# A hybrid decoder step: the delta rule's 32x32 blocks substituted on 128 partitions, from the right

## The chip, the cores and the metric

The kernel runs on one core of one Trainium2 chip. The metric is device time in microseconds of one execution; lower is better. Of the core's engines, PE (TensorE) multiplies matrices, DVE (VectorE) and ACT (ScalarE) work on elements, POOL (GpSimd) does small side work, and SP (SyncE) issues most of the DMA transfers. Each engine runs its own queue in order; semaphores tie the queues together.

## The reference

One layer of a decoder with two branches that read one input projection: a gated short convolution (A), and a gated DeltaNet (B) with 8 heads of 128 x 128. They are merged by sigmoid gates and projected out. There are 1024 prompt tokens and 8 samples of one token. The part that the change touches is the delta rule, which needs the inverse of a unit lower triangular matrix in every chunk of every head:

```
a_mat = jnp.where(strict, jnp.einsum('bhncd,bhnsd->bhncs', kb, k) * decay, 0.0)
a_mat = a_mat + jnp.eye(C, dtype=jnp.float32)
rhs = jnp.concatenate([v * beta[..., None], kb * jnp.exp(gc)[..., None]], axis=-1)
sol = lax.linalg.triangular_solve(a_mat, rhs, left_side=True, lower=True, unit_diagonal=True)
...
def step(S, xs):
    v_new = u_c - jnp.einsum('bhcd,bhde->bhce', w_c, S)
    o = jnp.einsum('bhcd,bhde->bhce', qd_c, S) + jnp.einsum('bhcs,bhse->bhce', aqk_c, v_new)
    S = S * gl_c[..., None, None] + jnp.einsum('bhcd,bhce->bhde', kd_c, v_new)
```

## The kernel before, in words

The input projection is a list of jobs of 128 columns each (`run`, line 692). A job has three groups of 344 tokens, each with 8 x 3 matmuls (`pm_t<-xh,whi`, `xl,whi`, `xh,wlo`: both sides are split in a high and a low part), which fill one of four PSUM tiles `pm`. ScalarE or VectorE then evacuates the tile. Weights come in as `wraw` two jobs ahead, and are split by ScalarE (`whi`) and VectorE (`wlo`).

Beside the projection, and between its matmuls, runs the work of the heads as strands (Python generators). `slot` (line 598) is called after every three matmuls and lets each strand whose due time is past issue its next piece. The due times come from a planner (`Sched`, line 60, and `Paced`, line 112): every instruction that is written advances a planned clock of its engine by a cost, a DMA by a latency and its size, and a strand is due when its last result is planned to be there. `sched.loose()` leaves an instruction out of the strand's own chain of due times. So a change of costs, of the number of instructions or of DMAs moves the order of all engines from that point on.

One strand per head is `delta_gen` (line 864). In its order:

- keys and queries (`kq`) are transposed and squared, and the products k·k and k·q of the 8 chunks of 128 tokens come in PSUM tiles `pa`; VectorE multiplies them by the decays into `DB` and `DA`. `DB` holds minus the strict lower triangle A.
- The four 32x32 diagonal blocks of each chunk, 32 blocks a head, go to DRAM (`sA<-DB`, line 935), and come back with one block per partition (`Tt<-sA`, line 942): 32 partitions of 1024 elements. The products `vp` and `qd` are made meanwhile.
- Lines 963 to 973 substitute: for j from 1 to 30, all rows below j add their element of column j times row j, in two VectorE instructions (`Ttmp<-Tt`, `Tt<-Tt,Ttmp`) of (31 - j) x j elements. The result is each block's inverse, whose diagonal is set to one in the middle.
- The inverse goes to DRAM (`sT<-Tt`, line 974) and comes back with rows on partitions (`Tn<-sT`, line 978). VectorE transposes it (`Un<-Tn`), ScalarE copies it into `U` and `T11`, and small matmuls (`Un,DB`, `Tn,Qs`, ...) build the 128x128 inverse.
- The chain over the 8 chunks follows: `X` (VectorE) from the product with the state, `U` x `X` (TensorE), `vn` (ScalarE), then the new state `S` (VectorE). At its end VectorE normalises the output `on`, and TensorE transposes it.

The chain of one head runs while the next head prepares its blocks. Two tiles `raw` hold projected queries, keys and values until VectorE has convolved them (`kq<-raw`, `vT<-raw`); until then the next columns wait in their PSUM tiles.

Of the kernel before, what the change touches and what calls it, by code (L numbers as in the profile page):

```python
# [8 lines left out]
F32 = mybir.dt.float32  # L9
# [3 lines left out]
ALU = mybir.AluOpType  # L13
# [3 lines left out]
P = 128  # L17
D = 1024
NK = 8
S = 1024  # L20
# [133 lines left out]
def hybrid_step(  # L154
# [8 lines left out]
    sched = Sched()  # L163
    V, A, PE, GP, SY = (Paced(e, n, sched) for e, n in (
        (nc.vector, "V"), (nc.scalar, "A"), (nc.tensor, "PE"), (nc.gpsimd, "GP"), (nc.sync, "SY")))
# [12 lines left out]
    def tt(out, a, b, op):  # L178
        V.tensor_tensor(out=out, in0=a, in1=b, op=op)
# [32 lines left out]
    def rsqrt1(x, n):  # L212

        col = lambda t: tp.tile([P, 1], F32, tag=f"rs_{t}", name=f"rs_{t}")[:n]
        y, a, x4, x16 = (col(t) for t in ("y1", "a1", "x4", "x16"))
        ts(y.bitcast(I32), x.bitcast(I32), -0.5, 1597463007.0, ALU.mult, ALU.add)
        ts(x4, x, 0.25)
        ts(x16, x, 0.0625)
        for xs_ in (x, x4, x16):
            ts(a, y, y, xs_, ALU.mult, ALU.mult)  # L220
            stt(y, a, 3.0, y, ALU.subtract, ALU.mult)
        return y
# [45 lines left out]
    sA = dram.tile([NH, NC, 4, 32, 32], F32, name="sA")  # L268
    sT = dram.tile([NH, NC, 4, 32, 32], F32, name="sT")
# [594 lines left out]
    def delta_gen(h, st):  # L864
# [13 lines left out]
        for src, sq in ((0, ssk), (1, ssq)):  # L878
            for half in range(2):
                pt = ps_aux()  # L880
                for i in range(4):
                    c = half * 4 + i
                    transpose(pt[:, i * C:(i + 1) * C], kq[:, src, c * C:(c + 1) * C])
                sched.loose()
                for i in range(4):
                    c = half * 4 + i
# [19 lines left out]
        for half in range(2):  # L906
# [7 lines left out]
            for c2 in (2 * half, 2 * half + 1):  # L914
# [6 lines left out]
                for i in range(2):  # L921
                    c = 2 * c2 + i
# [8 lines left out]
        t_kk = sched.cur.t  # L931
# [3 lines left out]
            SY.dma_start(out=sA[h, :, b].rearrange("c r j -> r c j"), in_=DB[bs, :, bs])  # L935
        while not T4.ready():
            yield
        Tt_ = T4.get("Tt", S)
        Tf = Tt_[:32]
        Tt = Tf.rearrange("p (r j) -> p r j", j=32)  # L940
        tmp = bp.tile([32, 256], F32, tag="Ttmp", name="Ttmp")
        SY.dma_start(out=Tt, in_=sA[h].rearrange("c b r j -> (c b) r j"))
        t_at, sched.cur.t = sched.cur.t, t_kk
        vp = bp.tile([P, NC, C], F32, tag="vp", name="vp", bufs=2)
        for half in range(2):
            pt = ps_aux()
            for i in range(4):
                c = half * 4 + i
# [11 lines left out]
        yield  # L960
        sched.cur.t = max(sched.cur.t, t_at)
        yield 0.0
        for j in range(1, 31):
            n = 31 - j
            tv = tmp[:, 0:n * j].rearrange("p (n w) -> p n w", w=j)
            tt(tv, Tt[:, j + 1:32, j:j + 1].to_broadcast([32, n, j]),
               Tt[:, j:j + 1, 0:j].to_broadcast([32, n, j]), ALU.mult)
            tt(Tt[:, j + 1:32, 0:j], Tt[:, j + 1:32, 0:j], tv, ALU.add)
            if j == 15:
                sched.loose()  # L970
                V.memset(Tf[:, 0:1024:33], 1.0)
                sched.loose(False)
            yield 0.0
        SY.dma_start(out=sT[h].rearrange("c b r j -> (c b) r j"), in_=Tt)
        T4.give(Tt_)
        Tn = bp.tile([P, NC, 32], F32, tag="Tn", name="Tn")
        Un = bp.tile([P, NC, 32], F32, tag="Un", name="Un")
        SY.dma_start(out=Tn, in_=sT[h].rearrange("c b r j -> (b r) c j"))
# [9 lines left out]
        for b in range(2):  # L988
            bs = slice(32 * b, 32 * b + 32)
            A.copy(out=T11[bs, :, bs], in_=Tn[bs])  # L990
        yield
# [8 lines left out]
        for p in (0, 1):  # L1000
# [13 lines left out]
            A.copy(out=U[b1, :, b2], in_=pt[b1, :, 0:32])  # L1014
            A.copy(out=T11[b2, :, 0:32], in_=pt2[b2, :, 0:32])
            yield 0.0
# [7 lines left out]
        for c in range(NC):  # L1024
            PE.matmul(pt[0:64, c, :], lhsT=T11[:, c, :], rhs=Qs[0:64, c, :], start=True, stop=True)
        A.copy(out=U[0:64, :, 64:128], in_=pt[0:64])
# [69 lines left out]
    def head_jobs(h):  # L1096
        st = {}

        def kdst():
            st["kq"] = bp.tile([P, 2, CY], F32, tag="kq", name="kq", bufs=2)  # L1100
            return st["kq"][:, 0, :]

        qkv_job(COL_K + h * P, 8 + h, lambda: h < 2 or flags.get(("done", h - 2)), kdst,
                lambda d: start(decay_gen(h, st)))
        qkv_job(COL_Q + h * P, h, lambda: "kq" in st, lambda: st["kq"][:, 1, :], lambda d: st.update(q=True))

        def vpost(d):
            st["v"] = d
            start(delta_gen(h, st))

        qkv_job(COL_V + h * P, 16 + h, lambda: "q" in st and T4.ready(), lambda: T4.get("vT", CY), vpost)

        return st
# [266 lines left out]
    def alloc(key, side):  # L1380
        pools[key] = tc.alloc_tile_pool(name=key, bufs=1, side=side)
        return pools[key]
# [369 lines left out]
    T4 = Slots(alloc("t4", "left"), "t4", NT4, CY)  # L1752
    bp = tc.alloc_tile_pool(name="bpool", bufs=1, side="left")
# [2 lines left out]
        GP.memset(r_[:, 0:3], 0.0)  # L1756
    U = bp.tile([P, NC, C], F32, name="U")
    T11 = bp.tile([64, NC, 64], F32, name="T11")
    GP.memset(U, 0.0)
    GP.memset(T11, 0.0)  # L1760
    for gi, (g0, gn) in enumerate(GROUPS):
# [55 lines left out]
    for j in range(9):  # L1817
        i, n, xr, mh, ml, held = pre.pop(j)
# [32 lines left out]
        r = rsqrt1(ms_[:n], n)  # L1851
        for half in range(2):
            hs = slice(half * 512, (half + 1) * 512)
            stt(yt[:n, hs], yt[:n, hs], r, xr[:n, hs], ALU.mult, ALU.add)
            out = y_prompt[0, i * P:(i + 1) * P, hs] if i < 8 else y_sample[:, 0, hs]
# [38 lines left out]
```

## Time and profile before

| | before |
|---|---|
| median of 3 runs | 1435.64 us (1431.11 to 1438.38) |
| span of the profiled execution | 1432.3 us |
| substitutions, VectorE busy, 8 heads | 76.1 + 76.2 us |
| granted TensorE clock, mean | 0.998 |

The profiled execution is known by its span, from its first to its last instruction; its own time is not listed apart from the runs. In the profile nearly every instruction has one line, that of the helper at line 121 that records it, so I go by the names of tiles: `out<-in`. A busy PE counts matmuls that overlap each other. "Idle ... <- X" is the time in which an engine had nothing running ahead of an instruction, and what ended it.

### The profile page before, as it was taken

The numbers are of one execution on the slowest core, as the hardware profiler recorded it, in microseconds if no ns is written. First come the engines' busy times: TensorE is split into PE (matmuls) and PEld (weight loads), VectorE is DVE, ScalarE is ACT, GpSimd is POOL, SyncE is SP. The second block draws the span as 40 slices with busy tenths as digits, with TensorE's granted clock in tenths as the row PEclk, the third lists the DMA queues.
The fourth block names the chain that finished last, engine by engine and source line by source line (L and its number), as shares of the span: only waits on it lengthen the run. The fifth ranks groups of instructions, "written<-read, shape, count | busy, mean of one in ns | idle before, by whom it ended". The sixth has DMA issues, their size and how long they took to land.

```text
span 1432.3 us, 25802 instructions
## 1 busy us (share of the span) xinstructions
PE 1401.0 (98%) x10130; PEld 1340.5 (94%) x10130; DVE 984.4 (69%) x2436; ACT 656.4 (46%) x1521; POOL 35.6 (2%) x59
## 2 busy tenths in 40 slices
PE   6999999899999999999999999999999999999997
PEld 4899999899999999999999999999999999999786
DVE  6754867759569585496864924988877867854553
ACT  6766453855528554466383332253323344532211
POOL 0000000100001000000000000000000110000000
PEclk9999999999999999999999999999999999999999
DMA  9523143132422324224132221344711885743221
GB/s 320 144 48 102 54 127 81 54 80 78 119 60 69 94 62 117 50 66 121 54 97 68 79 68 32 118 170 164 243 53 42 236 265 172 244 150 91 92 87 59
DMA packets 181922, 158.59 MB, mean 111 GB/s; under 512 B 25351, under 2 KB 157856, under 8 KB 181794
## 3 DMA queue, kind: packets, MB, share of 16 engines
q1 hardware_dynamic: 177248, 148.43, 35.2%
q0 software_dynamic: 4352, 8.46, 2.0%
q8 instruction: 79, 1.29, 0.4%
q14 instruction: 41, 0.34, 0.1%
q10 hardware_dynamic: 202, 0.08, 0.0%
HBM read 120.25 MB, written 36.91 MB: 110 GB/s over the span
## 4 chain that ended last, share of the span: by engine, by line
PE 84%; DVE 8%; DMA 5%; ACT 1%; issue 1%; SPq 1%; DVEq 0%; ACTq 0%
PE pm_t L121 63%; PE pa_t L121 19%; PE pb L121 2%; DVE acc L121 2%; DVE wlo L121 1%; DMA xs<-in_x_prompt_dram 1%; SPq L121 1%; DMA yraw<-yAsc 1%; DVE Tt L121 1%; DVE kq L121 1%; DMA wor<-in_w_o_dram 1%; DVE Ttmp L121 1%; DVE wr L121 0%; DMA yraw<-yBsc 0%; DMA pa__11678<-yBsc 0%
## 5 line engine op out<-in xcount | busy, mean ns | idle before, releaser
L121 PE MATMUL pm_t<-xh,whi 128*128 128x344 f32 (+1 forms) x1576 | 517.9, 329 | 2.2 <-ACT gate L121 2.2
L121 PE MATMUL pm_t<-xh,wlo 128*128 128x344 f32 (+1 forms) x1576 | 500.4, 318 | 0.0
L121 PE MATMUL pm_t<-xl,whi 128*128 128x344 f32 (+1 forms) x1576 | 500.1, 317 | 0.0
L121 PEld LDWEIGHTS pm_t<-xh,whi 128*128 128x128 f32 x1576 | 297.4, 189 | 4.7 <-ACT gate L121 2.5
L121 PEld LDWEIGHTS pm_t<-xl,whi 128*128 128x128 f32 x1576 | 297.3, 189 | 0.2
L121 PEld LDWEIGHTS pm_t<-xh,wlo 128*128 128x128 f32 x1576 | 296.9, 188 | 0.4
L121 DVE TENSOR_TENSOR wlo<-wraw,whi 128x512 fp32r<-128x512 f32 x136 | 91.8, 684 | 65.2 <-ACT whi L121 63.1
L121 ACT CAST whi<-wraw 128x512 fp32r<-128x512 f32 x136 | 82.7, 623 | 85.6 <-PE pm_t L121 83.6
L121 DVE TENSOR_TENSOR Ttmp<-Tt 32x30 f32<-32x30 f32 (+14 forms) x240 | 76.1, 317 | 14.7 <-DMA Tt<-sA 10.3
L121 DVE TENSOR_TENSOR Tt<-Tt,Ttmp 32x30 f32<-32x30 f32 (+14 forms) x240 | 76.2, 317 | 4.4
L121 ACT CAST whi<-wr 128x1024 fp32r<-128x1024 f32 x42 | 44.0, 1047 | 73.5 <-PE pa_t L121 34.9
L121 DVE SCALAR_TENSOR_TENSOR kq<-raw,vecs,kq 128x528 f32<-128x528 f32 x96 | 69.9, 758 | 1.5 <-ACT kq L121 1.3
L121 PE MATMUL pm_t<-thi,wlo 128*128 128x258 f32 x240 | 67.6, 283 | 1.6 <-DVE wlo L121 1.6
L121 PE MATMUL pm_t<-tlo,whi 128*128 128x258 f32 x240 | 67.6, 282 | 0.0
L121 PE MATMUL pm_t<-thi,whi 128*128 128x258 f32 x240 | 67.6, 282 | 0.0
L121 PE MATMUL pa_t<-thi,whi 128*128 128x258 f32 x224 | 63.3, 282 | 1.1 <-ACT whi L121 1.1
L121 PE MATMUL pa_t<-thi,wlo 128*128 128x258 f32 x224 | 63.4, 283 | 0.8 <-DVE wlo L121 0.8
L121 PE MATMUL pa_t<-tlo,whi 128*128 128x258 f32 x224 | 63.2, 282 | 0.0
L121 PE MATMUL pm_t<-yhi,whi 128*128 128x344 f32 x192 | 61.5, 321 | 0.0
L121 PE MATMUL pm_t<-ylo,whi 128*128 128x344 f32 x192 | 61.4, 321 | 0.0
L121 PE MATMUL pm_t<-yhi,wlo 128*128 128x344 f32 x192 | 61.4, 320 | 0.0
L121 DVE TENSOR_TENSOR wlo<-wr,whi 128x1024 fp32r<-128x1024 f32 x42 | 51.3, 1221 | 8.9 <-ACT whi L121 8.7
(406 smaller groups left out, 2834.0 us busy)
## 6 DMA issues: line engine op xcount, KB each, us to landing
wraw<-in_w_in_dram SPq DMA_DIRECT2D x60, 512.0 KB
wr<-in_w_in_dram SPq DMA_DIRECT2D x40, 256.0 KB
aw<-in_ada_w_dram SPq DMA_DIRECT2D x16, 512.0 KB
gBsc<-gate SPq DMA_DIRECT2D x8, 516.0 KB
gAsc<-gate SPq DMA_DIRECT2D x8, 516.0 KB
txs<-phi SPq DMA_DIRECT2D x8, 516.0 KB
txs<-plo SPq DMA_DIRECT2D x8, 516.0 KB
tlo<-txs POOLq DMA_DIRECT2D x8, 516.0 KB, 7.3
```

The lines of the kernel that those rows point to most:

```text
L121: r = f(*args, **kw)
```

## The change

The rows of the 32x32 blocks are dealt over four groups of 32 partitions: group g holds rows g, g + 4, g + 8, ... of all 32 blocks in a tile `Tw` (128 partitions, 8 rows of 32). `Tw` starts as the identity, copied by GpSimd from a constant `Ti`, and the blocks themselves are loaded four times, once for each group, into `At`. The substitution runs from the right: for j from 31 down to 1, each row adds its element of column j times row j of A to its columns below j. Only rows from 4 * (j // 4) on take part, so an instruction has (8 - j // 4) x j elements per partition, on 128 partitions. There are 31 steps of two instructions in place of 30. Four stores put the rows back in their places in `sT`. `Ttmp` has 80 elements in place of 256. The planned time of the loads now counts from the products (`t_kk`), not from the landing of the sA stores.

```
-        Tt_ = T4.get("Tt", S)
-        Tf = Tt_[:32]
-        Tt = Tf.rearrange("p (r j) -> p r j", j=32)
-        tmp = bp.tile([32, 256], F32, tag="Ttmp", name="Ttmp")
-        SY.dma_start(out=Tt, in_=sA[h].rearrange("c b r j -> (c b) r j"))
+        At_ = T4.get("At", S)
+        At = At_.rearrange("p (r j) -> p r j", j=32)
+        Tw = bp.tile([P, 8, 32], F32, tag="Tw", name="Tw")
+        tmp = bp.tile([P, 80], F32, tag="Ttmp", name="Ttmp")
+        GP.tensor_copy(out=Tw, in_=Ti)
+        sched.cur.t = t_kk
+        for g in range(4):
+            sched.loose(g < 3)
+            SY.dma_start(out=At[32 * g:32 * g + 32], in_=sA[h].rearrange("c b r j -> (c b) r j"))
...
-        for j in range(1, 31):
-            n = 31 - j
+        for j in range(31, 0, -1):
+            r0 = j // 4
+            n = 8 - r0
             tv = tmp[:, 0:n * j].rearrange("p (n w) -> p n w", w=j)
-            tt(tv, Tt[:, j + 1:32, j:j + 1].to_broadcast([32, n, j]),
-               Tt[:, j:j + 1, 0:j].to_broadcast([32, n, j]), ALU.mult)
-            tt(Tt[:, j + 1:32, 0:j], Tt[:, j + 1:32, 0:j], tv, ALU.add)
-            if j == 15:
-                sched.loose()
-                V.memset(Tf[:, 0:1024:33], 1.0)
-                sched.loose(False)
+            tt(tv, Tw[:, r0:8, j:j + 1].to_broadcast([P, n, j]),
+               At[:, j:j + 1, 0:j].to_broadcast([P, n, j]), ALU.mult)
+            tt(Tw[:, r0:8, 0:j], Tw[:, r0:8, 0:j], tv, ALU.add)
             yield 0.0
-        SY.dma_start(out=sT[h].rearrange("c b r j -> (c b) r j"), in_=Tt)
-        T4.give(Tt_)
+        T4.give(At_)
+        for g in range(4):
+            sched.loose(g < 3)
+            SY.dma_start(out=sT[h, :, :, g::4, :].rearrange("c b r j -> (c b) r j"), in_=Tw[32 * g:32 * g + 32])
...
+    Ti = bp.tile([P, 8, 32], F32, name="Ti")
+    GP.memset(Ti, 0.0)
+    for g in range(4):
+        GP.memset(Ti.rearrange("p r j -> p (r j)")[32 * g:32 * g + 32, g:g + 253:36], 1.0)
```

The order moves on every engine from head 0's substitution on. Three places follow.

VectorE, where head 4's first step stands among the chain of head 3 (`X` and `S`), before:

```order
L121 SCALAR_TENSOR_TENSOR S_5804<-S_5747,egl_96,pa_t_5801 128x128
L121 SCALAR_TENSOR_TENSOR X_5823<-pa_t_5819,nx_4427,vp_4741 128x128
L121 SCALAR_TENSOR_TENSOR S_5852<-S_5804,egl_96,pa_t_5849 128x128
L121 TENSOR_TENSOR Ttmp_5760<-Tt_5759 32x30
L121 MEMSET Tt_5759 32x32
L121 TENSOR_TENSOR Tt_5759<-Tt_5759,Ttmp_5760 32x30
L121 TENSOR_TENSOR Ttmp_5760<-Tt_5759 32x58
L121 SCALAR_TENSOR_TENSOR X_5870<-pa_t_5866,nx_4427,vp_4741 128x128
```

and now:

```order
L121 SCALAR_TENSOR_TENSOR S_5899<-S_5851,egl_96,pa_t_5896 128x128
L121 SCALAR_TENSOR_TENSOR X_5917<-pa_t_5913,nx_4457,vp_4709 128x128
L121 SCALAR_TENSOR_TENSOR S_5944<-S_5899,egl_96,pa_t_5941 128x128
L121 SCALAR_TENSOR_TENSOR X_5963<-pa_t_5959,nx_4457,vp_4709 128x128
L121 TENSOR_TENSOR Ttmp_5803<-Tw_5802,At_5801 128x31
L121 TENSOR_TENSOR wlo_6069<-wraw_5738,whi_6023 128x512
L121 TENSOR_TENSOR Tw_5802<-Tw_5802,Ttmp_5803 128x31
```

Counted from head 4's last `DA<-pa_t`, two `X` stood ahead of the first step and the third four rows behind it; now four stand ahead of it, and none follows within the next ten rows.

VectorE again, at the end of head 0's chain, where head 2's convolutions (`kq<-raw`) stand among the steps of the normalisation (`ro`) of head 0's output `on`; `Un` is head 1's, `DB` and `DA` are head 2's decays. Before:

```order
L121 SCALAR_TENSOR_TENSOR ro_y_2930<-ro_a_2931,ro_y_2930 128x8
L121 SCALAR_TENSOR_TENSOR kq_2924<-raw0_719,vecs_82,kq_2924 128x528
L121 TENSOR_TENSOR ro_a_2931<-ro_y_2930 128x8
L121 SCALAR_TENSOR_TENSOR kq_2924<-raw0_719,vecs_82,kq_2924 128x528
L121 SCALAR_TENSOR_TENSOR ro_a_2931<-ro_a_2931,so_2706 128x8
L121 SCALAR_TENSOR_TENSOR kq_2924<-raw1_720,vecs_82,kq_2924 128x528
L121 SCALAR_TENSOR_TENSOR ro_y_2930<-ro_a_2931,ro_y_2930 128x8
L121 SCALAR_TENSOR_TENSOR kq_2924<-raw1_720,vecs_82,kq_2924 128x528
L121 TENSOR_TENSOR on_2705<-on_2705,ro_y_2930 128x1024
L121 TENSOR_TENSOR DB_3091<-DA_3092,m_strict_72 128x1024
```

and now:

```order
L121 SCALAR_TENSOR_TENSOR kq_2933<-raw1_720,vecs_82,kq_2933 128x528
L121 TENSOR_TENSOR ro_a_2940<-ro_y_2939 128x8
L121 STREAM_TRANSPOSE Un_3024<-Tn_3023 128x256
L121 SCALAR_TENSOR_TENSOR ro_a_2940<-ro_a_2940,so_2515 128x8
L121 TENSOR_TENSOR DB_3043<-DA_3044,m_strict_72 128x1024
L121 SCALAR_TENSOR_TENSOR ro_y_2939<-ro_a_2940,ro_y_2939 128x8
L121 COPY qs_s_99<-kq_2933 128x8
L121 TENSOR_TENSOR DA_3044<-DA_3044,m_causal_77 128x1024
L121 TENSOR_TENSOR on_2514<-on_2514,ro_y_2939 128x1024
```

From the last `S` of the chain to `on` there were eleven `kq`; now there are nine, and `Un`, `DB` and `DA` stand ahead of `on`. On TensorE 37 projection matmuls stood between the chain's last product and the transposes of `on`; now 73 do.

SP's queue at head 1, from the stores of its blocks, before:

```order
L121 DMA sA_106<-DB_1754 32x8x32 x4
L121 DMA wraw_3149<-in_w_in_dram 128x8x128
L121 DMA Tt_2489<-sA_106 32x1024
L121 DMA rsc_113<-sm_rT_2595 8x128
L121 DMA rB_2297<-rsc_113 128x1024
```

and now:

```order
L121 DMA sA_106<-DB_1771 32x8x32 x4
L121 DMA At_2496<-sA_106 32x1024 x4
L121 DMA rsc_113<-sm_rT_2681 8x128
L121 DMA wraw_3074<-in_w_in_dram 128x8x128
L121 DMA rB_2392<-rsc_113 128x1024
```

Four loads stand where one stood, and the weight load that stood ahead of it stands behind them.

## The prediction

> **What bounds the kernel now.** I read the page first, then busy time by stage, then who waits on TensorE, then those places row by row.
>
> ```profile
> span 1432.3 us, 25802 instructions
> PE 1401.0 (98%) x10130; PEld 1340.5 (94%) x10130; DVE 984.4 (69%) x2436; ACT 656.4 (46%) x1521; POOL 35.6 (2%) x59
> PE 84%; DVE 8%; DMA 5%; ACT 1%; issue 1%; SPq 1%; DVEq 0%; ACTq 0%
> ```
>
> TensorE is busy 98% of the span and carries 84% of the chain; VectorE, the engine that the change relieves, is busy 69%. A faster VectorE is worth only what TensorE waits for it. The change touches the heads, so I cut the span where the heads begin and end and where TensorE idles. Columns: window, its length, busy time and count of PE, PEld, DVE, ACT, POOL, granted clock, DMA share, GB/s.
>
> ```profile
> 0.00:62.00 62.00, 48.87 (x308) 38.77 (x309) 42.86 (x109) 44.13 (x71) 5.12 (x21) 1.00 0.84 257
> 62.00:264.00 202.00, 202.00 (x1409) 195.63 (x1408) 132.41 (x388) 105.13 (x269) 1.63 (x6) 1.00 0.31 79
> 264.00:276.00 12.00, 8.06 (x77) 7.08 (x76) 12.00 (x28) 11.86 (x24) 2.89 (x2) 1.00 0.12 34
> 276.00:498.00 222.00, 221.95 (x1707) 214.36 (x1707) 155.75 (x457) 124.71 (x365) 7.61 (x7) 1.00 0.30 82
> 498.00:509.00 11.00, 9.00 (x53) 8.72 (x52) 5.24 (x22) 3.08 (x12) 0.00 (x0) 0.84 0.29 74
> 509.00:930.00 421.00, 421.00 (x3136) 411.92 (x3135) 286.50 (x831) 194.68 (x536) 6.74 (x7) 1.00 0.28 79
> 930.00:1433.00 503.00, 490.07 (x3452) 463.98 (x3450) 349.60 (x607) 172.83 (x249) 11.58 (x16) 1.00 0.46 147
> ```
>
> From 62 to 930 us, where all eight heads lie, TensorE idles 3.94 us in one place (264 to 276), 2.00 in another (498 to 509) and 0.05 elsewhere. In the second the granted clock is 0.84, which costs 0.16 x 11 = 1.8 us more. So **the room in the stage of the change is about 7.8 us**, 0.54% of the span. The 13.1 us idle before 62 and 12.9 after 930 lie outside the heads. TensorE's waits of the stage:
>
> ```profile
> PE pm_t L121 <- ACT gate L121: 2.2, 1, 2.2
> PE pa_t L121 <- DVE X L121: 2.0, 1, 2.0
> PE pa_t L121 <- DVE on L121: 1.7, 1, 1.7
> ```
>
> The place at 501 us (a timeline of VectorE, and the window behind it):
>
> ```profile
> 499.28 0.35 DVE L121 SCALAR_TENSOR_TENSOR S<-S,egl,pa_t 128x128 f32<-128x128 f32 x1 [2.20 <-PE pa_t L121]
> 502.81 0.19 DVE L121 TENSOR_TENSOR Ttmp<-Tt 32x30 f32<-32x30 f32 x1 [3.18 <-DMA Tt<-sA]
> 503.40 0.33 DVE L121 SCALAR_TENSOR_TENSOR X<-pa_t,nx,vp 128x128 f32<-128x128 f32 x1
> 503.80:508.40 4.60, 4.60 (x23) 4.60 (x23) 3.37 (x13) 1.24 (x5) 0.00 (x0) 0.63 0.00 0
> ```
>
> The first substitution step of head 4 stands at the front of VectorE's queue and waits 3.18 us for its DMA; X of head 3's chain is queued behind it, and TensorE waits for X. Afterwards the clock is 0.63 for 4.6 us: 0.37 x 4.6 = 1.7 us. **Price of this place: 2.0 + 1.7 = 3.7 us.**
>
> The place at 264 to 276 us (VectorE and TensorE):
>
> ```profile
> 263.04 0.35 DVE L121 SCALAR_TENSOR_TENSOR S<-S,egl,pa_t 128x128 f32<-128x128 f32 x1
> 271.97 1.21 DVE L121 TENSOR_TENSOR on<-on,ro_y 128x1024 f32<-128x1024 f32 x1
> 267.49 0.42 PE L121 MATMUL pm_t<-xh,whi 128*128 128x344 f32 x1 [2.22 <-ACT gate L121]
> 273.23 1.09 PE L121 MATMUL pa_t<-ident,on 128*128 128x128 f32 x8 [1.72 <-DVE on L121]
> 159.58 34.42 PE pm_t L121 x219
> L121 DVE SCALAR_TENSOR_TENSOR kq<-raw,vecs,kq 128x528 f32<-128x528 f32 x96 | 69.9, 758 | 1.5 <-ACT kq L121 1.3
> ```
>
> The last row but one is from the chain of waits: 34.42 / 219 = 0.157 us for each projection matmul. In the order of before, 37 of them stand between head 0's last chain product and the transposes of `on`: 5.8 us of work. VectorE needs 10.1 us from that S to the end of `on` (263.04 to 273.1), most of it eleven convolution instructions `kq` of 0.76 us. The difference, 4.3, is the 3.9 us that TensorE idles: once for a PSUM bank behind a full ScalarE, once for `on`. **Price: 3.9 us**, and the substitution is not in it (it ended at 258); only the order can change it.
>
> **The change, part by part.** *The substitution's instructions.*
>
> ```profile
> L121 DVE TENSOR_TENSOR Ttmp<-Tt 32x30 f32<-32x30 f32 (+14 forms) x240 | 76.1, 317 | 14.7 <-DMA Tt<-sA 10.3
> L121 DVE TENSOR_TENSOR Tt<-Tt,Ttmp 32x30 f32<-32x30 f32 (+14 forms) x240 | 76.2, 317 | 4.4
> L121 DVE TENSOR_TENSOR nx<-cB,egc 128x8 f32<-128x8 f32 x8 | 1.4, 173 | 0.2
> L121 DVE TENSOR_TENSOR Ttmp<-Tt 32x58 f32<-32x58 f32 x16 | 3.3, 207 | 0.5
> L121 DVE TENSOR_TENSOR Ttmp<-Tt 32x84 f32<-32x84 f32 x16 | 3.7, 231 | 0.4
> ```
>
> Before, 60 instructions a head, 152.3 / 8 = 19.0 us. Now 31 steps of two, each of (8 - j//4) x j elements per partition: 8 to 76, mean 1560 / 31 = 50. Eight elements on 128 partitions take 173 ns, 58 on 32 take 207, 84 take 231: the length counts, the partitions do not show. At 50 elements I take 200 ns, bounded by the 173 and 231: 62 x 0.200 = 12.4 us a head (10.7 to 14.3). VectorE loses 6.6 us a head, 53 us in all. On the path this is worth nothing by itself, since the three windows that hold all of the substitutions but the start of head 4's (62 to 264, 276 to 498, 509 to 930) have at most 0.05 us of idle TensorE; it counts through the two places.
>
> *The transfers.*
>
> ```profile
> 405.39 1.82 SPq L121 DMA_DIRECT2D sA<-DB  x4
> 408.45 0.31 SPq L121 DMA_DIRECT2D Tt<-sA  x1
> 185.60 0.32 SPq L121 DMA_DIRECT2D sT<-Tt  x1
> 187.64 0.41 SPq L121 DMA_DIRECT2D Tn<-sT  x1
> 192.73 0.45 DVE L121 STREAM_TRANSPOSE Un<-Tn 128x256 f32<-128x256 f32 x1 [0.88 <-DMA Tn<-sT]
> ```
>
> Four loads for one: 3 x 0.31 = 0.9 us more on SP, so `At` is complete 0.9 to 1.2 us later than `Tt` was. Four stores of 128-byte rows for one of 4 KB rows: the four sA stores, also of 128-byte rows, keep the next load waiting 3.06 us (405.39 to 408.45), the one sT store 2.04 (185.60 to 187.64); so `Tn` comes 1.0 us later, at most 7.1 + 1.0 = 8.1 us behind the last step. Behind SP's extra 1.9 us a head stand weight loads, issued two jobs (2 x 72 x 0.157 = 22.6 us) ahead: hidden; without that cover 1.9 us a head. For `Un` and the ScalarE copies of `Tn` the cover is the distance in the new order: at least 94 projection matmuls (14.8 us) between the last PSUM tile read ahead of the last step and the first product with `Un`. More than 8.1, so nothing.
>
> *The copy of the identity on GpSimd* is not shown before. Its nearest row is a copy of 24 elements:
>
> ```profile
> L121 POOL COPY raw<-hist_q x24: 197/262/3512, 59.5 to 715.7; 128x24 f32<-128x24 f32 x24
> ```
>
> From 0.2 to 3.5 us (least, median, most) for 24 elements; for 256 I bound it by 0.2 and 4 us and take 1. It is issued with the sA stores, some 5 us before `At` lands, and costs nothing; if that cover went, the first step and what VectorE has queued behind it would wait up to 4 us at a head. The setup memsets on GpSimd lie beside the first projection.
>
> *The order.* In the new order the first step of head 4 stands behind two more rounds of X and S of head 3's chain than before. Rounds there are about 4 us apart, so it comes some 8 us later, against 3.18 us of waiting plus 1.2 us of later landing: the wait goes. At the other heads X follows five rows behind the first step at the earliest, and the product that it reads is made later than `At` lands. Term: **-3.7 us** (at worst 0: the wait stays). At head 0's end 73 projection matmuls (11.5 us) now stand where 37 did; VectorE's queue there holds nine `kq` (6.9), `Un` (0.45), two wide decay instructions and `on` (1.2 each, as `on` above), 11.0 us, and half a microsecond of small ones. So the 3.9 us go if the queue keeps time: **-3.9 us**, bounds 0 and -3.9. This end is narrow, and counted the same way those of heads 2, 4 and 6 have 0.4 to 0.5 us to spare (before, heads 2 and 4 had 0.3 and 0.7, and no wait). I charge 0.5 us for each of the four: **+2.0 us**, bounds 0 and 4 x 2.
>
> **Sum:** -3.7 - 3.9 + 2.0 = -5.6 us, so the profiled span would go from 1432.3 to 1426.7. The span is 3.3 us under the median of the runs (1435.64) and inside them (1431.11 to 1438.38); I put the difference on the median: **1430.0 us**.
>
> **The rivals.**
> 1. *All room goes*: both waits vanish, no new one comes, and the shifted transfers after 930 us save a microsecond or two of 12.9. 1435.6 - 7.8 - 1.3 = 1426.5. For it: the counts above; against: four narrow ends.
> 2. *Nothing on balance*: one wait moves to another head, or the short instructions do not get shorter (the change then does not do what it says), and VectorE's load is as before: 1435.6. For it: the narrow ends. Against: the wait at 501 us is gone by a wide margin.
> 3. *Slower: the longer way through sT.* Should the last step run late against TensorE, so that less than 8.1 us lie between it and the first `Un` product, every head pays the 1.0 us of late `Tn` and, as at 503 us, part of a 1.7 us slow clock: 8 x (1.0 + 0.3) = 10.4, so 1446. Against: 14.8 us at the narrowest. The Trainium skill, "DMA: Bandwidth & Descriptors", Specifications, says that transfers under 512 B fall below line rate, with a read-modify-write, which speaks against the four stores. The sA row agrees only so far as 1.0 us.
> 4. *More room than idle time shows.* If TensorE's weight loads, not its matmuls, measure its room, the stage has 868.0 - 837.7 = 30.3 us (PEld of the five windows from 62 to 930), and a freed VectorE could give all of it: 1405. Against: 202.00 of 202 us are busy in a window whose PEld is 195.63, with nothing that waits. The Trainium skill, "Perfetto Trace Analysis", Identifying the Most-Contended Engine, has this rule: matmul busy time is a poor measure of the distance from the limit, weight-load busy share a better one.
>
> **How the numbers follow.** Forecast 0.44, rival 1 0.22, rival 2 0.25, rival 3 0.07, rival 4 0.02. 0.5%, about what a measurement of this kernel can tell from no change, is 7.2 us: below 1428.5 or above 1442.8. A quarter of the forecast's cases lie below 1428.5 (it is 1.5 us above), and nearly all of rival 1's: 0.11 + 0.20 + 0.02 = 0.33 faster; slower 0.08 (rival 3 and a little of rival 2); same 0.59. The range leaves out rivals 3 and 4 and the fringes of 1 and 2: 1422 to 1440.
>
> **What would show it.** Right: DVE busy falls by about 53 us to some 930, steps of 0.17 to 0.23 us; no PE wait for X near head 4's first step, clock 1.00 there; PE idle from 62 to 930 us about 2 us. Wrong: PE waits for `on` of 2 us at several heads, or for `Un`, U or X behind `At` or `Tn`; steps over 0.25 us; a low clock in a new place.

## The result, and the profile after

| | before | after |
|---|---|---|
| median of the runs | 1436.06 us (1431.11 to 1438.38) | 1422.88 us (1422.29 to 1424.44) |
| span of the profiled execution | 1432.3 us | 1420.6 us |
| substitutions, VectorE busy, 8 heads | 76.1 + 76.2 us | 51.9 + 51.9 us |

The ratio is 0.9909, 95% interval 0.9891 to 0.9926: 13.2 us faster, more than twice the 5.6 forecast. Three lines of the page of after (span, busy time, and the chain that ended last by engine):

```profile
span 1420.6 us, 25886 instructions
...
PE 1396.6 (98%) x10130; PEld 1341.2 (94%) x10130; DVE 937.7 (66%) x2444; ACT 658.0 (46%) x1521; POOL 36.5 (3%) x72
...
PE 91%; DVE 5%; DMA 3%; ACT 1%; SPq 0%; issue 0%; DVEq 0%; ACTq 0%
```

VectorE lost 46.7 us (984.4 to 937.7), but TensorE's sum of weight loads is the same (1340.5 and 1341.2) and its busy time fell by only 4.4 of the 11.7 us of the span. The windows of after, in the prediction's columns:

```profile
62.00:264.00 202.00, 201.97 (x1417) 197.12 (x1416) 128.47 (x412) 113.56 (x284) 3.31 (x10) 1.00 0.33 82
264.00:276.00 12.00, 11.95 (x149) 10.92 (x148) 8.67 (x16) 11.76 (x22) 0.20 (x1) 1.00 0.22 71
276.00:498.00 222.00, 221.93 (x1683) 217.27 (x1681) 140.99 (x454) 120.92 (x365) 5.68 (x8) 1.00 0.33 90
498.00:509.00 11.00, 11.00 (x76) 11.00 (x74) 10.83 (x59) 8.40 (x18) 0.00 (x0) 1.00 0.21 54
509.00:930.00 421.00, 420.51 (x3123) 411.29 (x3124) 269.42 (x809) 193.09 (x528) 9.60 (x10) 1.00 0.31 85
930.00:1433.00 503.00, 480.61 (x3387) 454.94 (x3385) 336.50 (x590) 166.11 (x237) 11.58 (x16) 0.99 0.45 143
```

From 62 to 930 us, TensorE idles 0.64 us (6.0 before). The two places are empty, and the clock at 498 to 509 us is 1.00. TensorE's waits that the profile shows between 62 and 930 us (total, times, longest) are these two, the first at the window's edge, and neither for `X`, `Un` or a gate:

```profile
PE pm_t L121 <- ACT last_q L121: 1.1, 1, 1.1
PE pa_t L121 <- DVE on L121: 0.5, 1, 0.5
```

At head 4 (a timeline of VectorE), `X` now runs first, and the first step behind it waits for nothing:

```profile
496.82 0.35 DVE L121 SCALAR_TENSOR_TENSOR X<-pa_t,nx,vp 128x128 f32<-128x128 f32 x1 [1.04 <-PE pa_t L121]
497.19 0.19 DVE L121 TENSOR_TENSOR Ttmp<-Tw,At 128x31 f32<-128x31 f32 x1
```

**Waits inside "busy".** Idle time went down by 7.3 us in the whole span, yet the span by 11.7. So I took the start of every matmul to the start of the next, less the 20th percentile of that interval for the same three neighbours (the matmul ahead, the matmul itself and the next, by PSUM tile and shape) over 15 traces: what is over is lost time, idle or not. Here is that sum by stage, in us:

| | before | after |
|---|---|---|
| ahead of 62 us | 10.8 | 11.0 |
| 62 to 930 us | 21.4 | 11.0 |
| of it waits over 1 us | 6.4 (3) | 0 |
| of it slow clock at 504 to 508 us | 1.7 | 0 |
| of it waits of 0.04 to 0.2 us ahead of products of the heads | 6.1 (70) | 2.8 (33) |
| of it waits of 0.2 to 1 us | 0.2 (1) | 1.1 (3) |
| after 930 us | 13.8 | 12.3 |

The four rows from 62 to 930 us name 14.4 of the 21.4 us before and 3.9 of the 11.0 after. The other 7 us in each are nearly all differences under 0.04 us, which a 20th percentile leaves in any order. The weight loads tell the same: from 62 to 930 us they are busy 837.7 us before and 847.6 after, so the time without one fell from 30.3 to 20.4 us, by 9.9, where idle time fell by 5.35.

The short waits look like this: a timeline of TensorE before, in head 0's chain, with two to four projection matmuls between the links, and VectorE's two rows of `S`.

```profile
252.15 0.32 PE L121 MATMUL pm_t<-xl,whi 128*128 128x344 f32 x1
252.30 0.61 PE L121 MATMUL pa_t<-S,kq 128*128 128x128 f32 x4
252.66 0.40 PE L121 MATMUL pm_t<-xh,wlo 128*128 128x344 f32 x1
...
253.97 0.49 PE L121 MATMUL pa_t<-vn,kd 128*128 128x128 f32 x2
254.30 0.39 PE L121 MATMUL pa_t<-vn,DA 128*128 128x128 f32 x2
254.44 0.40 PE L121 MATMUL pm_t<-xh,wlo 128*128 128x344 f32 x1
254.68 0.32 PE L121 MATMUL pm_t<-xh,whi 128*128 128x344 f32 x1
254.90 0.71 PE L121 MATMUL pa_t<-S,kq 128*128 128x128 f32 x4
255.37 0.40 PE L121 MATMUL pm_t<-xl,whi 128*128 128x344 f32 x1
...
251.63 0.35 DVE L121 SCALAR_TENSOR_TENSOR S<-S,egl,pa_t 128x128 f32<-128x128 f32 x1
254.50 0.35 DVE L121 SCALAR_TENSOR_TENSOR S<-S,egl,pa_t 128x128 f32<-128x128 f32 x1 [0.17 <-PE pa_t L121]
```

The same group takes 0.36 us to the next start at 252.30 and 0.47 at 254.90, where it stands only two projection matmuls behind the product that `S` is made from. The row is 0.1 longer, and the matmul ahead starts 0.22 before it, against 0.15. The `S` that it reads ends at 254.85, 0.05 us ahead of it; that of the group at 252.30 ended 0.32 ahead. Neither wait shows as idle, since the rows overlap.

### The profile page after: what moved, and what is told of

It is laid out like the page before. It is cut to its first block, busy times and chain, and to the rows that moved or that the text cites. A ratio compares the mean times of both kernels' runs of the same rounds, so it can differ in the third digit from the quotient of the medians.

```text
span 1420.6 us, 25886 instructions
## 1 busy us (share of the span) xinstructions
PE 1396.6 (98%) x10130; PEld 1341.2 (94%) x10130; DVE 937.7 (66%) x2444; ACT 658.0 (46%) x1521; POOL 36.5 (3%) x72
## 4 chain that ended last, share of the span: by engine, by line
PE 91%; DVE 5%; DMA 3%; ACT 1%; SPq 0%; issue 0%; DVEq 0%; ACTq 0%
PE pm_t L121 66%; PE pa_t L121 22%; PE pb L121 2%; DVE kq L121 1%; DMA xs<-in_x_prompt_dram 1%; DMA yraw<-yAsc 1%; DMA wor<-in_w_o_dram 0%; DVE S L121 0%; SPq L121 0%; DMA sg<-gAsc 0%; DVE wlo L121 0%; DVE Tw L121 0%; DVE Ttmp L121 0%; DMA sg<-gBsc 0%; DVE ml L121 0%
## 5 line engine op out<-in xcount | busy, mean ns | idle before, releaser
L121 DVE TENSOR_TENSOR Ttmp<-Tw,At 128x60 f32<-128x60 f32 (+24 forms) x248 | 51.9, 209 | 8.8 <-DMA At<-sA 3.7
L121 ACT ACTIVATE junk<-pa_t 128x128 f32<-128x128 f32 x192 | 53.8, 280 | 5.6 <-PE pa_t L121 2.7
```

Source lines behind the costliest of these rows:

```text
L121: r = f(*args, **kw)
```

## The experiments

Fifteen kernels ran. The kernel before, run beside them, gave 1436.4 to 1436.9 us in the medians of four batches.

**The old steps in the new order, and the new steps in the old.** The planner's figures are kept apart from the work: here it counts one substitution while the other is issued.

```
         for j in range(31, 0, -1):
+            for _ in range(2):
+                sched.note("V", 66.0 + (8 - j // 4) * j / 0.96)
+            sched.mute = True
+            i = 31 - j
+            n = 31 - i
...
+                tt(tv, Tt[:, i + 1:32, i:i + 1].to_broadcast([32, n, i]),
+                   Tt[:, i:i + 1, 0:i].to_broadcast([32, n, i]), ALU.mult)
+                tt(Tt[:, i + 1:32, 0:i], Tt[:, i + 1:32, 0:i], tv, ALU.add)
...
+            sched.mute = False
```

> The changed kernel with the 60 substitution instructions of before put back (on partitions 0 to 31), while the planner goes on counting the 62 short ones, and the four loads and four stores stay: new order, old VectorE time (about 19.0 us a head in place of 13.0). Theory O (the order is what brings the gain: the two places and the short waits go because instructions stand elsewhere): as the changed kernel, 1422 to 1426 us, TensorE idle 62 to 930 us under 1.5 us. Theory W (VectorE's shorter queue brings it: X, S and vn come sooner because each step ahead of them is shorter): back to 1433 to 1437 us. A half each: about 1429.

Measured: 1433.24 us (1428.09 to 1442.54), ratio 0.9982 (0.9962 to 1.0002). The two places are gone (11.65 busy of 12 us, 11.00 of 11), but TensorE's waits from 62 to 930 us are new ones:

```profile
PE pm_t L121 <- DVE wlo L121: 2.6, 4, 1.8
PE pa_t L121 <- DVE Un L121: 1.8, 2, 1.4
PE pa_t L121 <- DVE DA L121: 0.9, 1, 0.9
```

So neither theory: the new order alone keeps some 3 of 13 us, and the interval takes in none. The clock has a part in that: the eight runs with a mean clock of 0.996 to 0.998 have the median 1430.9, the four of 0.990 to 0.992 lie at 1437.9 to 1442.5. A second edit was in this kernel: `At` is here what is stored to `sT`, so the pool slot's next user waits for that store, which VectorE does for 3.6 us ahead of `kql`. The double products below are without it. The next kernel turns the exchange round:

```
+        for i in range(1, 31):
+            for _ in range(2):
+                sched.note("V", 66.0 + (31 - i) * i / 0.96)
...
+            sched.mute = True
+            for j in ((31, 30) if i == 1 else (31 - i,)):
...
+                tt(Tw[:, r0:8, 0:j], Tw[:, r0:8, 0:j], tv, ALU.add)
+            sched.mute = False
```

> The kernel before with the 62 short steps, four loads and four stores, while the planner goes on counting the 60 old ones: the planner's order of before. Only the first step of head 4 stands two chain rounds later than before (after 28 X in place of 26), as in the changed kernel, and 46 projection matmuls (37 before, 73 after) stand at the end of head 0's chain. Theory O: the place at 501 us goes (-3.7), that at 264 to 276 us keeps 3.9 - 9 x 0.157 = 2.5 us of idle TensorE, the short waits stay: 1430 to 1433 us. Theory W: 1422 to 1426 us.

Measured: 1436.07 us (1434.11 to 1441.63), ratio 0.9999 (0.9987 to 1.0010): nothing. At the places it went as theory O had it (idle 12 - 9.48 = 2.5 us at 264 to 276, none at 498 to 509), but its time was missed by 3 us, and theory W falls by 10. The profiled execution is the slowest of the twelve runs, 5.6 us over their median. By its matmul starts it loses 8.2 us in short waits (94) in the heads, 4.2 us by a clock of 0.52 for 10.2 us behind the first place, and 17.7 us after 930. So the short waits stay with the new steps in the old order; where the median run loses what the place at 501 us gave is not shown.

```profile
264.00:276.00 12.00, 9.48 (x83) 8.68 (x82) 12.00 (x28) 11.84 (x25) 2.90 (x2) 0.95 0.03 8
...
274.40:284.60 10.20, 10.20 (x103) 9.70 (x103) 6.11 (x14) 7.72 (x14) 0.07 (x1) 0.52 0.13 54
...
498.00:509.00 11.00, 11.00 (x82) 11.00 (x81) 3.01 (x8) 2.66 (x11) 0.00 (x0) 1.00 0.69 165
```

**One load for four.** This was meant to put head 4's first step back to its old place.

```
-        for g in range(4):
-            sched.loose(g < 3)
-            SY.dma_start(out=At[32 * g:32 * g + 32], in_=sA[h].rearrange("c b r j -> (c b) r j"))
+        SY.dma_start(out=At, in_=sA[h].rearrange("c b r j -> (c b) r j").unsqueeze(0).to_broadcast([4, 32, 32, 32]))
...
+        SY.dma_start(out=sT[h].rearrange("c b (r g) j -> g (c b) r j", g=4), in_=Tw)
```

> The changed kernel with one load and one store in place of four each; the planner counts them so. The order hardly moves, but the first step of head 4 stands after 26 X again, where it stood before the change. Theory O: the stall at about 501 us is back and costs 3 to 4 us: 1425 to 1428 us. Theory W: the place of one instruction decides nothing, and the shorter transfers save up to 1 us: 1421 to 1424 us.

> As the run before it, but At is loaded by one transfer that reads sA four times over, and sT written by one; the first step of head 4 then stands after 26 X, where it stood before the change. Theory O: the stall at about 501 us is there as before the change (2 us of idle TensorE, VectorE waiting about 3 us for At), and most of the one at 264 to 276: 1433 to 1437 us. Theory W: 1422 to 1427 us.

Measured: 1482.70 us, ratio 1.0321 (1.0302 to 1.0339), and 1478.33 us, ratio 1.0297 (1.0279 to 1.0316). Both theories missed, since the transfer is another one. In the first of the two kernels, timelines of SP, VectorE and TensorE at head 4:

```profile
526.92 0.55 SPq L121 DMA_DIRECT2D At<-sA  x1
535.56 0.19 DVE L121 TENSOR_TENSOR Ttmp<-Tw,At 128x31 f32<-128x31 f32 x1 [10.12 <-DMA At<-sA]
536.12 0.34 DVE L121 SCALAR_TENSOR_TENSOR X<-pa_t,nx,vp 128x128 f32<-128x128 f32 x1
536.51 0.80 PE L121 MATMUL pa_t<-X,U 128*128 128x128 f32 x2 [8.90 <-DVE X L121]
```

A window of it while the load runs, and one of after behind its four loads for head 0 (DMA share and GB/s last):

```profile
528.00:534.00 6.00, 0.00 (x0) 0.00 (x0) 0.00 (x0) 0.00 (x0) 0.00 (x0) 0.77 0.26 82
```

```profile
143.00:147.00 4.00, 4.00 (x28) 4.00 (x27) 1.03 (x9) 2.02 (x6) 0.00 (x0) 1.00 0.79 207
```

The one load takes 8.6 us from issue to first step, on 0.26 of the DMA engines; with the four, issued from 141.27 us on, head 0's first step starts at 147.67, 6.4 us later, on 0.79, though a weight load of 512 KB, issued at 140.70, shares that window. The Trainium skill, "DMA: Bandwidth & Descriptors", Rules for kernel authors, says that a leading zero-stride broadcast of c copies confines a transfer to at most c of 16 engines: 4 of 16 is 0.25, and the trace's 0.26 agrees. In all, VectorE stands 58.3 us at the first steps of all eight heads, waiting for `At` (3.7 in after), with the chain queued behind them. TensorE idles 45.3 us from 62 to 930 us (0.6 in after), 20.7 of them in five waits for `X`, at a mean clock of 0.98, which is some 17 us more by estimate (0.02 x 868); the kernel is 59.8 us slower than after. The one store is laid out with a count of 4 in front as well, but TensorE waits nowhere for `Un`. The order hardly moved (about 1% of TensorE's rows), but the first steps stand up to two rounds of the chain earlier, where such a wait meets them. This is the mechanism of the place at 501 us, the late `X` and the slow clock, made larger.

**Other orders of the same work.** `SLK`, the slack with which a strand falls due, is changed by a few per cent, and with it the order on every engine.

```
-SLK = 450.0
+SLK = 430.0
```

> The kernel before with the planner's slack at 430 ns in place of 450: the same work in another order (2349 of 9275 TensorE instructions moved, about as many as the change moves). Theory C (each order draws its own stalls, and the change's gain is mostly such a draw): anywhere from 1425 to 1445 us, with places of idle TensorE of 1.5 to 4 us somewhere else than at 264 and 501 us; here 70 projection matmuls stand at the end of head 0's chain, so that place should be gone. Theory M (an order fits the work it was planned with, and the shorter work makes any order better): 1433 to 1439 us, as before.

> The kernel before with slack 470 ns (2538 of 9275 TensorE instructions moved; 51 projection matmuls at the end of head 0's chain). Theory C: 1425 to 1445 us, and not the same as with 430. Theory M: 1433 to 1439 us.

> The changed kernel with slack 430 ns (1943 of 9275 TensorE instructions moved). Theory C: 1418 to 1438 us, overlapping the orders of the kernel before. Theory M: 1420 to 1427 us, 9 to 15 us under the kernel before whatever the order.

> The changed kernel with slack 470 ns (774 of 9275 TensorE instructions moved). Theory C: 1418 to 1438 us. Theory M: 1420 to 1427 us.

> The kernel before with slack 400 ns (2176 of 9275 TensorE instructions moved against 450). Theory D, formed on the four runs ahead of this one: the change is worth about 7.5 us on the mean of many orders, and each order draws some 4 us to either side of its kernel's mean (before 1433, changed 1426); the change's own -13.2 us holds about 6 us of such a draw. D expects 1429 to 1437 us here. Theory M (the whole 13 us is the shorter work, the draw is small): 1434 to 1438 us.

> The kernel before with slack 500 ns (2652 moved). Theory D: 1429 to 1437 us. Theory M: 1434 to 1438 us.

> The changed kernel with slack 400 ns (1945 moved). Theory D: 1422 to 1430 us. Theory M: 1420 to 1425 us.

> The changed kernel with slack 500 ns (1844 moved). Theory D: 1422 to 1430 us. Theory M: 1420 to 1425 us.

Medians in us, with the ratio to the kernel before:

| slack | before | changed |
|---|---|---|
| 400 | 1427.03, 0.9935 (0.9920 to 0.9951) | 1429.44, 0.9949 (0.9931 to 0.9967) |
| 430 | 1435.20, 0.9995 (0.9975 to 1.0015) | 1427.06, 0.9941 (0.9919 to 0.9963) |
| 450 | 1436.06, 1 | 1422.88, 0.9909 (0.9891 to 0.9926) |
| 470 | 1428.60, 0.9952 (0.9935 to 0.9968) | 1427.41, 0.9944 (0.9923 to 0.9964) |
| 500 | 1433.29, 0.9970 (0.9956 to 0.9985) | 1425.36, 0.9926 (0.9909 to 0.9943) |
| mean | 1432.0 | 1426.4 |

Theory C holds in all four of its ranges, which are 20 us wide. Theory M falls by orders of the old work at 1427.0 and 1428.6 and one of the new at 1429.4. Theory D, formed in between, missed one of four, by 2 us. The five differences, from +2.4 to -13.2, have the mean -5.6 and a standard error of 2.8 us (6.2 between pairs, over the root of 5). Five are few: the 95% interval of that mean is -13.3 to +2.1, and -10.6 to -0.6 if the two columns are compared without pairing, since one slack draws two unrelated orders. By the matmul starts, the time lost from 62 to 930 us is 21.1 us in the mean of the five orders before (15.0 to 29.8) and 15.5 in those of the change (11.0 to 17.6). The 29.8 is slack 430, profiled 8 us over its median with a slow clock that cost 13.7; without it the mean before is 18.9. **Over orders the change is worth some 6 us by the best estimate, which is not secured; the rest of its 13 is then the draw of this pair**: the order of before is the slowest of its five, that of after the fastest. The old work at slack 400 has 9 of the 13 us without the change.

**VectorE's work alone, with the plan kept.** The first leaves out 30 of a head's 31 steps, the third the last 10 of the old kernel's 30, and the planner counts them all the same; the second writes each product twice, and the planner counts it once:

```
+            sched.mute = True
+            tt(tv, Tw[:, r0:8, j:j + 1].to_broadcast([P, n, j]),
+               At[:, j:j + 1, 0:j].to_broadcast([P, n, j]), ALU.mult)
+            sched.mute = False
```

> The changed kernel with its plan kept (78 of 9275 TensorE instructions moved); of the 31 substitution steps of a head only the first is done, the rest of the inverse is left out: VectorE some 101 us less. If VectorE's length decides (theory L, slope by the first pair 13.2 / 46.7 = 0.28 us a us): 1395 us. If it decides only where TensorE waits for it (theory P), what is left to gain is the excess of short waits of 100 to 930 us beyond the best, some 3 us: 1418 to 1423 us.

> The changed kernel with its plan kept (456 of 9275 moved) and the product of each step written twice: 93 in place of 62 instructions a head, VectorE some 52 us more, about its time in the kernel before, and all transfers and buffers as in the changed kernel. Theory L: back by 0.28 x 52 = 14 us, about 1437 us. Theory P: 1424 to 1431 us, with waits for Un or wlo where the chain is now late. Theory O (only the order counts): 1421 to 1424 us.

> The kernel before with its plan kept (178 of 9275 moved) and the last ten of the 30 steps of a head left out: VectorE some 45 us less, transfers as before. Theory L: 1436 - 0.28 x 45 = 1423 us. Theory P: the places at 264 and 501 us are not of the length of the steps, so 1432 to 1436 us, as the new steps in the old order gave 1436.

Measured: 1424.27 us, ratio 0.9910 (0.9895 to 0.9925), the same as after; 1431.03 us, 0.9963 (0.9948 to 0.9977), 8 us over after; 1437.28 us, 1.0004 (0.9991 to 1.0017), the same as before. Pages of the three (busy time), and TensorE's waits from 62 to 930 us where steps were left out of the old kernel:

```profile
PE 1397.6 (98%) x10130; PEld 1341.6 (94%) x10130; DVE 862.7 (61%) x1964; ACT 658.5 (46%) x1521; POOL 39.0 (3%) x72
```

```profile
PE 1401.1 (98%) x10130; PEld 1341.3 (94%) x10130; DVE 971.1 (68%) x2692; ACT 658.2 (46%) x1521; POOL 34.5 (2%) x72
```

```profile
PE 1404.0 (98%) x10130; PEld 1342.4 (94%) x10130; DVE 947.7 (66%) x2276; ACT 660.2 (46%) x1523; POOL 33.2 (2%) x59
```

```profile
PE pm_t L121 <- ACT gate L121: 2.6, 1, 2.6
PE pa_t L121 <- DVE X L121: 2.4, 1, 2.4
PE pm_t L121 <- ACT raw L121: 1.1, 1, 1.1
...
```

Theory L falls twice: 75 us less VectorE (937.7 to 862.7) gain nothing in the new order, and 37 us less (984.4 to 947.7) nothing in the old, whose two places stay where they were. (The rows of the steps sum to more, but overlap with others.) Theory O falls by 1431.0. Theory P comes nearest, though 1424.3 and 1437.3 us lie 1.3 us over its ranges and 1431.03 on the edge of its third: VectorE's time counts only where TensorE waits for it. In the other direction it counts: with 33 us more work (971.1) the new order gives back 8 of its 13 us, by the matmul starts 5.7 of them in the heads: 3.1 in short waits (70 of 6.0 us, after 33 of 2.8) and 2.2 in waits of 0.2 to 1 us. **With steps longer than it was planned with, the new order loses most of its gain.**

## Why the prediction was right in its places and wrong in its size

- *The place at 501 us, -3.7:* right. Lost time by matmul starts from 500 to 600 us went from 4.5 to 0.9 us, and the wait, the slow clock and the late `X` are gone. The margin was smaller than thought: the step now stands 14.1 us behind the issue of head 4's blocks (483.12 to 497.19), where VectorE had come to it 8.7 behind (490.90 to 499.63), so 5.3 us later and not some 8, against a wait of 3.2. The kernel with one load shows the same mechanism made larger.
- *The place at 264 to 276 us, -3.9:* right; its idle time is gone. "The substitution is not in it" is shown by the old kernel with ten steps left out, which keeps 3.7 us of waits there. "Only the order can change it" holds as well: the new steps in the old order, with 46 projection matmuls there for 37, kept 2.5 us, as 3.9 - 9 x 0.157 has it.
- *New waits at four narrow ends, +2.0:* too much. One came, 0.5 us for `on`; all waits of 0.2 to 1 us rose by 0.9.
- *The step that failed:* "**the room in the stage of the change is about 7.8 us**", read from idle time and the clock. By the starts of matmuls, 21.4 us were lost there before. Of the 10.4 that went, 8.1 are those two places (6.4 in waits over 1 us and 1.7 of slow clock); 3.3 are short waits of 0.04 to 0.2 us, which the windows count as busy; 0.9 came back in middle ones. The window from 62 to 264 us was full, 202.00 of 202, but not free of waits: the piece of head 0's chain quoted above lies in it. The sum held no term for such waits. They need the short steps: written twice, the products bring 3.1 us of them back.
- *Outside the sum:* 1.5 us less was lost after 930 us, of which the forecast had nothing and rival 1 had 1.3. And the profiled execution stood 3.8 us under the median before, 2.3 after: 1.5 more. With 0.2 more ahead of 62 us: -10.4 - 1.5 - 1.5 + 0.2 = -13.2, as measured. To the forecast's -5.6 this adds 1.1 of new waits that did not come (2.0 - 0.9), 3.3 of short waits, 1.5 and 1.5; the two places were 0.5 larger than thought.
- *What the range stood on:* waits that move. The largest term of uncertainty was not among them: orders of one and the same work lie 9.0 us apart before and 6.6 after. That the forecast meets the mean over orders (-5.6) is luck: its terms were for this order.
- *Rival 4, more room than idle time shows:* right in its measure, wrong in its size. The sum of weight loads is nearly the same in these kernels (1340.5 us before, 1341.2 after, 1349.3 in the one 60 us slower), so their share of the span follows the time: 93.6, 94.4 and 91.2%. From 62 to 930 us the time without a weight load fell by 9.9 us, where the forecast's measure, idle time, fell by 5.35. So the rule that it names (the Trainium skill, "Perfetto Trace Analysis", Identifying the Most-Contended Engine), a weight-load share before matmul busy time, is borne out here, except for a slow clock, which stretches the loads too (1355.1 us at slack 430 of the old work). But VectorE could not give all of the 30.3 us: 20.4 are left in after, and 21.0 with nearly no steps.
- *Rival 3, the longer way through sT:* did not come. `Un` starts 7.4 to 10.5 us behind the last step at seven heads and 16.6 at one, at all but one beyond the "at most 8.1" of the prediction, but TensorE waits for it nowhere in after; in the old steps in the new order it does (1.8 us).
- *The steps:* 0.200 us predicted, 0.209 measured, 13.0 us a head for 12.4; VectorE's busy time 937.7 for some 930, so 46.7 us went and not 53. In groups by line of after (busy, mean ns, idle ahead):

```profile
L121 DVE TENSOR_TENSOR Ttmp<-Tw,At 128x60 f32<-128x60 f32 (+24 forms) x248 | 51.9, 209 | 8.8 <-DMA At<-sA 3.7
L121 DVE TENSOR_TENSOR Tw<-Tw,Ttmp 128x60 f32<-128x60 f32 (+24 forms) x248 | 51.9, 209 | 4.9
L121 POOL COPY Tw<-Ti 128x256 f32<-128x256 f32 x8 | 3.8, 479 | 175.8 <-DMA sT<-Tw 101.8 <-DVE ro_a L121 74.0
```

- *GpSimd's copy of the identity:* 0.48 us for 1, hidden as said. *At:* four loads, and VectorE waits 3.7 us for them in all, TensorE for none of it.
- *"On the path worth nothing by itself":* right for the old order, twice over, and for any step shorter still; but the new order needs the shorter steps to keep its gain.

No order tried beats the changed kernel's own 1422.9 us, and with nearly no steps left it runs at 1424.3: in this order, the substitution has nothing more to give.

## What to carry to other kernels

Where a planner orders the work, a change of costs is also a new draw of the order: change a constant of the planner by a few per cent on both kernels, and judge the change by the mean and its error, before explaining a per cent. Full busy windows are not free of waits where matmul rows overlap: the time without a weight load shows how much they sum to, and the intervals between starts, compared with the same neighbours elsewhere, show where they are. Work taken off an engine beside the path is worth what the path waits for it, but an order planned for the shorter work needs it short.

## What the runs showed of the hardware that was not expected

**A late operand costs about 0.1 us that no row calls idle**, as at 254.90 us above; 70 waits of that length were 6.1 us.

**The clock's price differs from one execution to the next.** In the profiled execution of the old work at slack 430 the granted clock was 0.52 for 14 us and 0.54 for 18.5, worth 0.48 x 14 + 0.46 x 18.5 = 15.2 us, or 13.7 by the starts of matmuls. Before the first the profile shows no wait, before the second one of 0.71 us, ahead of a stretch with many 32x32 products (windows, and TensorE's timeline):

```profile
412.00:426.00 14.00, 14.00 (x75) 13.02 (x75) 3.41 (x14) 1.96 (x6) 0.00 (x0) 0.52 0.18 48
...
480.00:498.50 18.50, 18.50 (x131) 17.00 (x131) 5.87 (x22) 10.03 (x45) 0.00 (x0) 0.54 0.07 29
```

```profile
477.40 0.69 PE L121 MATMUL pa_t<-Un,DB 32*32 32x32 f32 x16 [0.71 <-DVE Un L121]
```

The ten runs of that kernel span 1429.7 to 1441.7 us: five with a mean clock of 0.993 or 0.994 lie at 1429.7 to 1431.2, five of 0.985 to 0.991 at 1435.4 to 1441.7. The twelve runs of the old steps in the new order part in the same way. The Trainium skill, "TensorE: Matmul & The Clock Gate", HAM oscillation, puts the fall of the clock to idle gaps over some 3.4 us; here it came with none that long, and did not come behind the gaps of 2.2 and 1.7 us at 264 to 276 us of before, but did behind 2.5 us of idle time at the same place of the new steps in the old order. What sets it off here stays open. The changed kernel has no such stretch between 62 and 930 us, and its four runs lie within 2.2 us.

**One transfer that reads the same source four times** kept 0.26 of the DMA engines busy, and brought 512 KB in 8.6 us where four transfers, beside a weight load of 512 KB, took 6.4 from the first one's issue.
